# A ring of twelve 14 KB weight slots in place of twenty-one 8 KB slots, with whole-row reads of the expert matrices

## The chip, the cores and the metric

One core of one Trainium2 chip runs the kernel. The metric is device time in microseconds (us) of one execution. Engines are named as in the profile: PE (TensorE matmul), PEld (its weight loads), DVE (VectorE), ACT (ScalarE), POOL (GpSimd) and SP (SyncE), which issues nearly all DMAs. L148 is line 148 of the kernel before.

## The reference

A two-layer backbone over 256 latent and 256 context tokens of width 1024, in float32. Layer 0 is attention beside a convolution module and then a dense feed-forward network; layer 1 is a state-space mixer and then a mixture of experts over the 256 latent tokens alone:

```python
logits = (hf @ w_router).astype(jnp.float32)
top_v, top_i = lax.top_k(logits, TOP_K)              # 2 of 8
gates = ...                                          # softmax of the two, zero elsewhere
for e in range(N_EXPERTS):                           # w1, w3: 1024 x 3584, w2: 3584 x 1024
    out = out + gates[:, e:e + 1] * swiglu(hf, w1[e], w3[e], w2[e])
```

`swiglu` is (silu(h w1) * (h w3)) w2. A final RMSNorm follows. Each matrix of an expert has 14.68 MB, an expert 44.04 MB, all eight 352.3 MB.

## The kernel before

**Order of the program.** Phases 1 and 2 compute layer 0 and the mixer of layer 1 (to about 1052 us in the profile). `route` picks the two experts of each token, `gather` (L1486, L1492, L1494) collects the tokens of an expert as columns of `xe`, and `experts` runs the eight experts. Experts 1 to 7 are taken in an order by token count, with fixed room for 3, 2, 3, 2, 3, 2, 3, 1 groups of 32 tokens (`GROUPS`); call that the number of groups.

**An expert.** The 3584 hidden columns are cut in two slices, 4 x 512 columns and 4 x 384 columns (`SS`). `up(s, i, name)` multiplies the tokens with slice s of w1 (i = 0) or w3 (i = 1): for each of the 8 blocks of 128 rows, and for each group, four matmuls side by side in the four column strips of the array (L1533). ACT takes the silu of the first product (L1541), DVE multiplies it by the second (L1544). `turn(s)` transposes the result (L1566), `down(s)` multiplies it with the rows of w2 (L1598). `evict` copies the sums, `scatter` (L1622, L1627) adds them to the tokens. Order within expert e: both up of slice 0, scatter of expert e-1, turn(0), both up of slice 1, gather of expert e+1, turn(1), down(0), down(1).

**The weight pieces and their ring.** A piece is one DMA on SP's queue (L148). Up pieces are 128 rows by 2048 columns (1 MiB, runs of 8 KB) or by 1536 columns (0.75 MiB, runs of 6 KB); down pieces are 1 MiB with two rows of w2 per partition (runs of 8 KB), two pieces of each expert with two separate rows (runs of 4 KB). An expert has 32 up pieces and 14 down pieces. They go round 21 slots of 8 KB a partition: one of its own (`rawe`), nine of `t8p`, three of `rawp`, three of `hlp`, five of `rawm`; each piece, of whatever size, takes one slot, and a slot is free again when the last matmul that reads it is done. `AHEAD` is how many pieces are asked for ahead of the one in use.

**What is in that room in phase 2.** Kilobytes a partition, in order of address: `cp` 11, `rawp` 24, (`rawe` 8), `hlp` 24, `t8p` 72, `ecp` 5, `op` 22, `wp2` 48. `rawp` and `hlp` hold the raw and the split weights of the mixer's output projection, `t8p` its inputs and `g1`, which the residual reads (L806); `ecp` holds `cs` and `op` holds `BT` and `CT`, all read by the router's matmul (L1345); `wp2` holds small work tiles, the last of them read at L1357. `mp`, `rp` and `ep` (routing and expert work tiles) are opened over the room of closed pools: by default a new pool's first use waits for all tiles of the closed pools it overlaps.

**Queues.** An engine runs its instructions in order; that order is written at compile time by a list scheduler from simulated times. SP holds a DMA back until its slot is free and until a DMA eight before it has landed. `km` (slot numbers and group ranks, needed by `places`, L1659) and `g2r` are small DMAs in SP's queue (L1415, L1462).

Of the kernel before, what the change touches and what calls it, by code (L numbers as in the profile page):

```python
# [10 lines left out]
F32 = mybir.dt.float32  # L11
# [79 lines left out]
class Net:  # L91
# [31 lines left out]

    BUFS = {"t8": 9, "t2": 6, "pe": 9, "cv": 4, "g": 3}

# [10 lines left out]
    def load(self, view, pool=None):  # L136

        if isinstance(view, View):
            view = view.get()
        pieces = view if isinstance(view, list) else [(slice(0, P), view)]  # L140
        kk, n = pieces[0][1].shape[1:]
        if pool == "t8":
            t = self.wk([P, 2048], "t8")
# [5 lines left out]
        return v  # L149

    def wparts(self, v, k0, m, scale=None):
# [1355 lines left out]
    def pos_rows(self, pos):  # L1507

        nc = self.nc
        self.pos = pos  # L1510
        pt = self.ps()
        nc.tensor.transpose(pt[:16, 0:P], pos.rearrange("p b e -> p (b e)"), self.ident)
        r = self.wk([16, P], "posr", bufs=1)
        nc.scalar.copy(r, pt[:16, 0:P])
        d = self.drp.tile([16, P], F32, name=self.nm("posd"))
        nc.sync.dma_start(d, r)
        self.posd = d.rearrange("(b e) p -> b e p", b=2)

    def expert(self, e, n_g):
# [3 lines left out]

        def up(s, i, name):
            c0, n = self.SS[s]

            def begin():
                st[i] = [self.ps("h") for _ in range(n_g)]

            def mm(k, wv, _):  # L1530
                for g in range(n_g):
                    for p in range(4):
                        nc.tensor.matmul(st[i][g][32 * p:32 * p + 32, :n], st["x"][:, k, 32 * g:32 * g + 32],  # L1533
                                         wv[:, n * p:n * p + n], start=k == 0, stop=k == KD - 1,
                                         tile_position=(0, 32 * p))

            def end():
                if i == 0:
                    st["g"] = [self.wk([P, 512], "g")[:, :n] for _ in range(n_g)]
                    for g in range(n_g):  # L1540
                        nc.scalar.activation(st["g"][g], st[0][g][:, :n], AF.Silu)  # L1541
                else:
                    for g in range(n_g):
                        nc.vector.tensor_mul(st["g"][g], st["g"][g], st[1][g][:, :n])  # L1544

            view = lambda k: self.weights(name, e, [P, 1, 4 * n], lambda w: w[:, k * P:(k + 1) * P, c0:c0 + 4 * n]
                                          .rearrange("o p n -> p o n"))
            return Unit([view(k) for k in range(KD)], mm, begin, end, False)

        def take():  # L1550
            st["x"] = self.xe

        def turn(s):


            n = self.SS[s][1]

            def call():
                st["hT", s] = hT = self.wk([P, n // P, 3, P], f"hT{s}", bufs=1)
                for g in range(n_g):  # L1560
                    pt = self.ps("h")
                    for c in range(n // P):
                        t = st["g"][g][:, c // 2 * 256:c // 2 * 256 + min(256, n - c // 2 * 256)]
                        if t.shape[-1] == 256:
                            t = t.rearrange("p (i j) -> p j i", j=2)[:, c % 2]
                        nc.tensor.transpose(pt[:, c * P:(c + 1) * P], t, self.ident)  # L1566
                    o, i = hT[:, :n // P, g], pt[:, :n].rearrange("p (c t) -> p c t", t=P)
                    if g % 2:
                        nc.vector.tensor_copy(o, i)
                    else:  # L1570
                        nc.scalar.copy(o, i)
            return Unit(begin=call)

        def down(s):
            r0, n = 4 * self.SS[s][0] // 4, self.SS[s][1]
            rows = lambda r, m: (lambda w: w[:, r:r + m])
            pair = lambda w: w.rearrange("o (i j) n -> i (o j) n", j=2)
# [12 lines left out]
            def begin():  # L1590
                if s == 0:
                    st["y"] = [self.ps("y") for _ in range(0, n_g, 2)]

            def mm(k, wv, _):
                p, c = pieces[k // 2][1][k % 2]
# [8 lines left out]
            return Unit([self.weights("od_ex_w2", e, [P, 2, D], f) for f, _ in pieces], mm, begin,  # L1604
                        evict if s else None, False)
# [9 lines left out]
        def scatter():  # L1615
# [8 lines left out]
            for b in range(2):  # L1624
# [61 lines left out]
    def experts(self, n_g, now=None):  # L1686
# [21 lines left out]

    AHEAD = 20

# [9 lines left out]
    def moe(self):  # L1720
# [4 lines left out]
        self.run(self.experts(GROUPS, self.late), self.AHEAD)  # L1725
        self.fn = self.wk([P, D], "t8")
        nc.sync.dma_start(self.fn, self.A["final_norm"].partition_broadcast(P))
        self.o = self.wk([P, 2, D], "t8")
        self.finish()

        with self.tc.If(self.over > 0):
            self.rings = [self.rawp]
            for q in (0, 1):
# [10 lines left out]
    def finish(self):  # L1744

        nc = self.nc
        for b in range(2):
            for half in range(2):
                self.sumsq(2 + b, half, "g")
            rs = self.rms_rs(slice(2 + b, 3 + b))  # L1750
# [79 lines left out]
def build(tc, A, out, dbg=None):  # L1830
# [5 lines left out]

    with ExitStack() as ctx, tc.tile_pool(name="cp", bufs=1) as net.cp, \
            tc.tile_pool(name="rawp", bufs=3) as net.rawp, \
            tc.tile_pool(name="rawe", bufs=1) as net.rawe, \
            tc.tile_pool(name="hlp", bufs=3) as net.hlp:  # L1840
        net.drp = ctx.enter_context(tc.tile_pool(name="drp", bufs=1, space=bass.MemoryType.DRAM))
        with tc.tile_pool(name="t8p", bufs=9) as net.t8p, ExitStack() as early:
            net.ecp = early.enter_context(tc.tile_pool(name="ecp", bufs=1))
            with tc.tile_pool(name="xcp", bufs=1) as net.xcp, tc.tile_pool(name="rawx", bufs=1) as net.rawx, \
# [8 lines left out]
            early.close()  # L1853
            with psum("psm", h=6, y=2) as net.psp, tc.tile_pool(name="mp", bufs=1) as net.mp:
                net.t_tag = "h"
                with tc.tile_pool(name="rp", bufs=1) as net.wp:
                    net.route()
                with tc.tile_pool(name="ep", bufs=1) as net.wp, tc.tile_pool(name="rawm", bufs=5) as rawm:
                    net.rings = [net.rawe] + ["t8"] * 9 + [net.rawp] * 3 + [net.hlp] * 3 + [rawm] * 5
                    net.n_ring = -1  # L1860
                    net.moe()

# [12 lines left out]
```

## Time and profile before

| | us |
|---|---|
| median of 3 runs | 1911.31 (1908.12 to 1911.62) |
| the profiled execution | 1911.85 |
| its span | 1910.1 |
| PE busy | 1778.9 (93%) |
| DVE, ACT, POOL busy | 703.5, 519.1, 174.1 |
| read from HBM | 494.45 MB, 259 GB/s over the span |

The span runs from the first to the last profiled instruction; the profiled execution's own time has 1.75 us around it. Matmuls overlap and their ends are modelled, so a busy PE need not be working at its peak. A float32 matmul is two records. Where PE waits between two groups of matmuls, the row says in brackets how long and for whom.

### The profile page before, as it was taken

How to read it: one execution, taken by the hardware profiler on the slowest of the kernel's cores; microseconds unless marked ns; L12 is line 12 of the kernel's file. 1: busy time of each engine (PE TensorE's matmuls, PEld its weight loads, DVE VectorE, ACT ScalarE, POOL GpSimd, SP SyncE). 2: the span in 40 equal slices, each digit the busy share in tenths (PEclk: the TensorE clock that was granted, in tenths of full speed). 3: DMA queues.
4: the chain of work that ended last, by engine and by line, in shares of the span. 5: the costliest groups of instructions: out<-in, count | busy, mean ns of one | idle time of the engine just before them, and what ended most of it. 6: DMA issues, size and time to landing. Idle time of an engine off the chain costs nothing. (4 is left out here: it accounts for less than half of the span.)

```text
span 1910.1 us, 33591 instructions
## 1 busy us (share of the span) xinstructions
PE 1778.9 (93%) x14384; PEld 1110.9 (58%) x14384; DVE 703.5 (37%) x1143; ACT 519.1 (27%) x969; POOL 174.1 (9%) x167
## 2 busy tenths in 40 slices
PE   6999998999999989989989999999999999899964
PEld 3675356788888868757667445445644463435411
DVE  3395546334334356798887110101110101002001
ACT  3434454231222335756874100100000000001000
POOL 0064000000000014133320000000000000000000
PEclk8999999999999999989899899999999999999976
DMA  8543765422323243323357899999999999999995
GB/s 319 178 157 120 250 184 189 135 96 89 109 89 98 81 142 103 122 84 115 101 197 279 320 399 418 416 418 416 418 416 417 417 417 412 414 419 413 417 413 230
DMA packets 131574, 497.87 MB, mean 261 GB/s; under 512 B 11312, under 2 KB 18392, under 8 KB 102744
## 3 DMA queue, kind: packets, MB, share of 16 engines
q1 hardware_dynamic: 126808, 487.25, 66.3%
q10 hardware_dynamic: 4608, 8.39, 1.3%
q8 instruction: 115, 1.88, 0.4%
q14 instruction: 43, 0.35, 0.1%
HBM read 494.45 MB, written 1.15 MB: 259 GB/s over the span
## 5 line engine op out<-in xcount | busy, mean ns | idle before, releaser
L1533 PE MATMUL h<-raw,xe 128*32 128x512 f32 (+1 forms) x2664 | 265.6, 551 | 15.8 <-DMA raw<-in_od_ex_w_dram 15.8
L244 PE MATMUL g<-t,whl 128*128 128x512 f32 (+1 forms) x608 | 237.4, 390 | 0.0
L243 PE MATMUL g<-t,whl 128*128 128x512 f32 (+1 forms) x608 | 234.8, 396 | 2.1 <-ACT opad L1057 1.9
L245 PE MATMUL g<-t,whl 128*128 128x512 f32 (+1 forms) x608 | 232.7, 390 | 0.8 <-POOL whl L164 0.8
L1533 PE MATMUL h<-t,xe 128*32 128x384 f32 (+1 forms) x2200 | 214.9, 543 | 7.7 <-DMA t<-in_od_ex_w_dram 7.7
L164 DVE TENSOR_TENSOR whl<-raw,whl 128x1024 fp32r<-128x1024 f32 x109 | 137.7, 1266 | 206.6 <-ACT whl L161 206.1
L161 ACT CAST whl<-raw 128x1024 fp32r<-128x1024 f32 x129 | 134.5, 1049 | 269.9 <-PE g L245 234.3
L1533 PEld LDWEIGHTS h<-raw,xe 128*32 128x32 f32 x2664 | 97.8, 111 | 175.2 <-issue 113.2
L1544 DVE TENSOR_TENSOR g<-g,h 128x512 f32<-128x512 f32 (+1 forms) x38 | 23.6, 621 | 425.9 <-PE h L1533 238.6
L244 PE MATMUL g<-whl,t 128*128 128x512 f32 (+1 forms) x432 | 168.0, 392 | 9.2 <-DVE whl L164 7.3
L245 PE MATMUL g<-whl,t 128*128 128x512 f32 (+1 forms) x432 | 164.4, 389 | 0.0
L243 PE MATMUL g<-whl,t 128*128 128x512 f32 (+1 forms) x432 | 160.5, 394 | 1.9 <-DVE t L641 1.8
L1533 PEld LDWEIGHTS h<-t,xe 128*32 128x32 f32 x2200 | 79.1, 110 | 136.1 <-issue 91.8
L1598 PE MATMUL y<-raw,hT 128*32 128x256 f32 x2512 | 144.7, 388 | 9.7 <-DMA raw<-in_od_ex_w_dram 9.7
L1541 ACT ACTIVATE g<-h 128x512 f32<-128x512 f32 (+1 forms) x38 | 20.7, 544 | 448.9 <-PE h L1533 448.9
L243 PEld LDWEIGHTS g<-t,whl 128*128 128x128 f32 x608 | 116.6, 192 | 29.3 <-ACT opad L1057 2.3
L244 PEld LDWEIGHTS g<-t,whl 128*128 128x128 f32 x608 | 116.3, 191 | 23.7 <-issue 1.0
L245 PEld LDWEIGHTS g<-t,whl 128*128 128x128 f32 x608 | 115.4, 190 | 24.2 <-POOL whl L164 1.0
L428 POOL TENSOR_SCALAR rsv<-sst 128x1 f32<-128x1 f32 (+1 forms) x15 | 4.7, 311 | 1295.0 <-DVE sst L421 1294.8
L1598 PEld LDWEIGHTS y<-raw,hT 128*32 128x32 f32 x2512 | 80.0, 112 | 72.4 <-DMA raw<-in_od_ex_w_dram 15.0
L1598 PE MATMUL y<-t,hT 128*32 128x256 f32 x1744 | 103.4, 395 | 10.7 <-DMA t<-in_od_ex_w_dram 10.7
L1612 DVE TENSOR_TENSOR ys<-y,g2r 128x512 f32<-128x512 f32 (+1 forms) x12 | 6.6, 577 | 260.6 <-PE y L1598 260.6
(349 smaller groups left out, 2091.1 us busy)
## 6 DMA issues: line engine op xcount, KB each, us to landing
raw<-in_od_ex_w_dram SPq DMA_DIRECT2D x138, 1024.0 KB, 18.0
t<-in_od_ex_w_dram SPq DMA_DIRECT2D x102, 1024.0 KB, 19.2
raw<-in_od_ex_w_dram SPq DMA_DIRECT2D x68, 768.0 KB, 15.0
t<-in_od_ex_w_dram SPq DMA_DIRECT2D x60, 768.0 KB, 15.8
raw<-in_ev_ff_w_dram SPq DMA_DIRECT2D x32, 1024.0 KB, 5.1
raw<-in_ev_ada_w_dram SPq DMA_DIRECT2D x24, 1024.0 KB, 6.7
raw<-in_od_ada_w_dram SPq DMA_DIRECT2D x24, 1024.0 KB, 5.2
raw<-in_od_w_in_dram SPq DMA_DIRECT2D x20, 1024.0 KB, 5.2
```

The costliest lines, as they stand in the source:

```text
L161: self.nc.scalar.copy(hv, v[:, k0:k0 + m])
L164: eng.tensor_tensor(lv, v[:, k0:k0 + m], hv.bitcast(F32), op=ALU.subtract)
L243: mm(out, l[0], r[0], start=start, stop=False)
L244: mm(out, l[0], r[1], start=False, stop=False)
L245: mm(out, l[1], r[0], start=False, stop=stop)
L428: nc.gpsimd.tensor_scalar(v[:, :m], ss, inv_n, EPS, op0=ALU.mult, op1=ALU.add)
L1533: nc.tensor.matmul(st[i][g][32 * p:32 * p + 32, :n], st["x"][:, k, 32 * g:32 * g + 32], wv[:, n * p:n * p + n], start=k == 0, stop=k == KD ...
L1541: nc.scalar.activation(st["g"][g], st[0][g][:, :n], AF.Silu)
L1544: nc.vector.tensor_mul(st["g"][g], st["g"][g], st[1][g][:, :n])
L1598: nc.tensor.matmul(st["y"][g // 2][32 * q:32 * q + 32, g % 2 * 256:g % 2 * 256 + 256], st["hT", s][:, c, g, 32 * p:32 * p + 32], wv[:, 256 ...
L1612: nc.vector.tensor_tensor(ys[:, g:g + m], st["y"][g // 2][:, :256 * m].rearrange("p (g n) -> p g n", g=m), self.g2.unsqueeze(1).to_broadca ...
```

## The change

The pools `rawp`, `hlp`, `t8p` and `ecp` are closed after phase 2, `rawe` and `rawm` are gone, and a pool `big` of twelve slots of 14 KB a partition is opened in their place, with waits by tile: a slot waits only for the tiles that lay where it lies. An up piece is now 128 whole rows of w1 or w3 (1.75 MiB, runs of 14 KB), both slices at once; a down piece has two rows per partition in slice 0 (1 MiB, runs of 8 KB, 8 pieces) and three in slice 1 (1.5 MiB, runs of 12 KB, 4 pieces). An expert has 16 up pieces and 12 down pieces. Order within expert e: both up, scatter of expert e-1, gather of expert e+1, turn(0), turn(1), down(0), down(1). `AHEAD` goes from 20 to 12. `g` is a tile per slice, the row of positions shares the tile `prow`, and the final norm's vector and the output use slots s3 and s4.

```diff
-        def up(s, i, name):
-            c0, n = self.SS[s]
-
+        def up(i, name):
             def begin():
-                st[i] = [self.ps("h") for _ in range(n_g)]
+                st[i] = [[self.ps("h") for _ in self.SS] for _ in range(n_g)]
 
             def mm(k, wv, _):
                 for g in range(n_g):
-                    for p in range(4):
-                        nc.tensor.matmul(st[i][g][32 * p:32 * p + 32, :n], st["x"][:, k, 32 * g:32 * g + 32],
-                                         wv[:, n * p:n * p + n], start=k == 0, stop=k == KD - 1,
-                                         tile_position=(0, 32 * p))
+                    for s, (c0, n) in enumerate(self.SS):
+                        for p in range(4):
+                            nc.tensor.matmul(st[i][g][s][32 * p:32 * p + 32, :n], st["x"][:, k, 32 * g:32 * g + 32],
+                                             wv[:, c0 + n * p:c0 + n * p + n], start=k == 0, stop=k == KD - 1,
+                                             tile_position=(0, 32 * p))
...
-            view = lambda k: self.weights(name, e, [P, 1, 4 * n], lambda w: w[:, k * P:(k + 1) * P, c0:c0 + 4 * n]
+            view = lambda k: self.weights(name, e, [P, 1, 3584], lambda w: w[:, k * P:(k + 1) * P]
                                           .rearrange("o p n -> p o n"))
...
+        RJ = (2, 3)
...
             for p in range(4):
-                for c in range(n // 256):
-                    f = rows(r0 + n * p + 256 * c, 256)
-                    pieces.append((lambda w, f=f: pair(f(w)), [(p, 2 * c), (p, 2 * c + 1)]))
-            if n % 256:
-                for p in (0, 2):
-                    f = rows(r0 + n * p, 2 * n)
-                    pieces.append((lambda w, f=f: f(w).rearrange("o (s i) n -> i (o s) n", s=2)[n - P:n],
-                                   [(p, n // P - 1), (p + 1, n // P - 1)]))
+                for c in range(n // (m * P)):
+                    r = r0 + n * p + m * P * c
+                    pieces.append((lambda w, r=r: w[:, r:r + m * P].rearrange("o (i j) n -> i (o j) n", j=m),
+                                   [(p, m * c + j) for j in range(m)]))
...
-        return ([Unit(begin=take), up(0, 0, "od_ex_w1"), up(0, 1, "od_ex_w3")],
-                [turn(0), up(1, 0, "od_ex_w1"), up(1, 1, "od_ex_w3")], [turn(1), down(0), down(1)],
+        return ([Unit(begin=take), up(0, "od_ex_w1"), up(1, "od_ex_w3")], [turn(0), turn(1), down(0), down(1)],
                 Unit(begin=scatter))
...
-            a, b, c, d = self.expert(e, n_g[e])
-            units += a + scatter + b + gather(e + 1) + c
+            a, b, d = self.expert(e, n_g[e])
+            units += a + scatter + gather(e + 1) + b
...
-    AHEAD = 20
+    AHEAD = 12
...
-                with tc.tile_pool(name="ep", bufs=1) as net.wp, tc.tile_pool(name="rawm", bufs=5) as rawm:
-                    net.rings = [net.rawe] + ["t8"] * 9 + [net.rawp] * 3 + [net.hlp] * 3 + [rawm] * 5
+        with psum("psm", h=6, y=2) as net.psp, \
+                tc.tile_pool(name="big", bufs=1, reuse_waits="tile") as net.big, \
+                tc.tile_pool(name="mp", bufs=1) as net.mp:
+            net.t_tag = "h"
+            for i in range(12):
+                net.slot_tile([P, 3584], f"s{i}")
+            with tc.tile_pool(name="rp", bufs=1) as net.wp:
+                net.route()
+            with tc.tile_pool(name="ep", bufs=1) as net.wp:
+                net.rings = [f"s{i}" for i in (4, 5, 6, 7, 3, 8, 9, 11, 10, 0, 1, 2)]
```

## Rows read from the trace of the kernel before

**Rows 1.** The page: DMA busy tenths of 40 slices, all packets by size, instruction queues.
```profile
DMA  8543765422323243323357899999999999999995
...
DMA packets 131574, 497.87 MB, mean 261 GB/s; under 512 B 11312, under 2 KB 18392, under 8 KB 102744
...
q8 instruction: 115, 1.88, 0.4%
q14 instruction: 43, 0.35, 0.1%
```

**Rows 2.** Windows: start:end, length, busy PE, PEld, DVE, ACT, POOL, PEclk, DMA share, GB/s.
```profile
1066.00:1110.00 44.00, 44.00 (x397) 14.50 (x390) 5.22 (x22) 4.15 (x7) 0.00 (x0) 0.97 0.84 294
1110.00:1141.00 31.00, 31.00 (x384) 12.64 (x387) 1.22 (x2) 2.13 (x5) 0.00 (x0) 1.00 1.01 419
1141.00:1889.00 748.00, 705.61 (x8965) 342.25 (x8961) 73.22 (x170) 39.81 (x82) 0.00 (x0) 0.97 1.01 414
```

**Rows 3.** Waits of SP's queue, 1066 to 1112 us: us in total, times, longest.
```profile
SPq L148 <- PE h L1533: 25.4, 11, 6.9
```

**Rows 4.** Timeline of PE, 1056 to 1150 us (expert 0): start, us, instruction, count.
```profile
1065.20 4.46 PE L1533 MATMUL h<-raw,xe 128*32 128x512 f32 x24
1069.49 18.20 PE L1533 MATMUL h<-t,xe 128*32 128x512 f32 x168
...
1108.71 1.75 PE L1566 MATMUL h<-ka,g 128*128 128x128 f32 x12
1110.39 11.82 PE L1533 MATMUL h<-raw,xe 128*32 128x384 f32 x144
...
1141.49 3.79 PE L1486 MATMUL h<-pm,h 128*128 128x64 f32 x32
...
1146.28 4.09 PE L1598 MATMUL y<-raw,hT 128*32 128x256 f32 x72
```

**Rows 5.** Timeline of PE, 1780 to 1850 us (up pieces of expert 7).
```profile
1810.07 1.07 PE L1533 MATMUL h<-raw,xe 128*32 128x512 f32 x8 [1.42 <-DMA raw<-in_od_ex_w_dram]
...
1824.99 1.74 PE L1533 MATMUL h<-t,xe 128*32 128x512 f32 x8 [0.57 <-DMA t<-in_od_ex_w_dram]
...
1832.49 0.85 PE L1533 MATMUL h<-t,xe 128*32 128x384 f32 x8 [0.21 <-DMA t<-in_od_ex_w_dram]
...
1849.48 0.85 PE L1533 MATMUL h<-raw,xe 128*32 128x384 f32 x8 [1.03 <-DMA raw<-in_od_ex_w_dram]
```

**Rows 6.** Timelines of PE: last down piece of expert 3 and of expert 7.
```profile
1463.27 1.93 PE L1598 MATMUL y<-raw,hT 128*32 128x256 f32 x32 [0.60 <-DMA raw<-in_od_ex_w_dram]
...
1891.29 1.93 PE L1598 MATMUL y<-raw,hT 128*32 128x256 f32 x16 [1.45 <-DMA raw<-in_od_ex_w_dram]
```

**Rows 7.** Timeline, 1045 to 1070 us: the last readers of g1, CT and wp2's tiles.
```profile
1047.25 0.74 DVE L806 SCALAR_TENSOR_TENSOR yt<-g,rs,t 128x512 f32<-128x512 f32 x1
...
1050.98 0.64 PE L1345 MATMUL t<-CT,cs 128*32 128x256 f32 x8
...
1052.81 0.36 DVE L1357 SCALAR_TENSOR_TENSOR L<-t,rs,rbias 128x8 f32<-128x8 f32 x2 [0.70 <-PE t L1351]
```

**Rows 8.** Timeline of SP's DMA issues, 970 to 1070 us.
```profile
1034.33 0.84 SPq L148 DMA_DIRECT2D t<-in_od_ex_w_dram  x2
...
1051.71 0.33 SPq L1415 DMA_DIRECT2D km<-in_kc_dram  x1
```

**Rows 9.** DMA issues, 1066 to 1112 us: count, KB each, median us to landing.
```profile
t<-in_od_ex_w_dram SPq DMA_DIRECT2D x9, 768.0 KB, 4.4
```

**Rows 10.** DMA packets of 1360 to 1380 us and of 1286 to 1306 us.
```profile
DMA packets 1144, 8.36 MB, mean 418 GB/s; under 512 B 126, under 2 KB 126, under 8 KB 126
...
DMA packets 1508, 8.32 MB, mean 416 GB/s; under 512 B 167, under 2 KB 167, under 8 KB 1471
```

**Rows 11.** Timeline of DVE, 1058 to 1068 us.
```profile
1062.92 0.38 DVE L1494 TENSOR_SCALAR xe<-h,m2o,ac 128x96 f32<-128x96 f32 x1 [2.89 <-ACT xe L1492]
1063.22 0.20 DVE L1659 TENSOR_TENSOR ranked<-rank,km 128x49 f32<-128x49 f32 x1
```

More of the change, by code (lines that the diff above doesn't have):

```diff
@@ L122, in ps @@
         return self.psp.tile([P, 512], F32, tag=tag, name=self.nm(tag), bufs=self.psum_tags.get(tag))
-    BUFS = {"t8": 9, "t2": 6, "pe": 9, "cv": 4, "g": 3}
+    BUFS = {"t8": 9, "t2": 6, "pe": 9, "cv": 4, "g0": 3}
     def wk(self, shape, tag, dt=F32, bufs=None, pool=None):
@@ L141, in load @@
         kk, n = pieces[0][1].shape[1:]
-        if pool == "t8":
-            t = self.wk([P, 2048], "t8")
+        if isinstance(pool, str):
+            t = self.slot_tile([P, 3584], pool)
         else:
@@ L149, in load, with slot_tile @@
         return v
+    def slot_tile(self, shape, tag):
+        return self.big.tile(shape, F32, tag=tag, name=self.nm(tag))
     def wparts(self, v, k0, m, scale=None):
@@ L1512, in pos_rows @@
         nc.tensor.transpose(pt[:16, 0:P], pos.rearrange("p b e -> p (b e)"), self.ident)
-        r = self.wk([16, P], "posr", bufs=1)
+        r = self.wk([P, 256], "prow", bufs=1)[:16, :P]
         nc.scalar.copy(r, pt[:16, 0:P])
@@ L1522, in expert @@
         st = {}
-        def up(s, i, name):
-            c0, n = self.SS[s]
+        def up(i, name):
             def begin():
-                st[i] = [self.ps("h") for _ in range(n_g)]
+                st[i] = [[self.ps("h") for _ in self.SS] for _ in range(n_g)]
             def mm(k, wv, _):
                 for g in range(n_g):
-                    for p in range(4):
-                        nc.tensor.matmul(st[i][g][32 * p:32 * p + 32, :n], st["x"][:, k, 32 * g:32 * g + 32],
-                                         wv[:, n * p:n * p + n], start=k == 0, stop=k == KD - 1,
-                                         tile_position=(0, 32 * p))
+                    for s, (c0, n) in enumerate(self.SS):
[3 more added lines that the diff above has]
+                                             tile_position=(0, 32 * p))
             def end():
                 if i == 0:
[L1539 to L1544, printed above, removed]
-            view = lambda k: self.weights(name, e, [P, 1, 4 * n], lambda w: w[:, k * P:(k + 1) * P, c0:c0 + 4 * n]
+                    st["g"] = [[self.wk([P, n], f"g{s}", bufs=3) for s, (_, n) in enumerate(self.SS)]
+                               for _ in range(n_g)]
+                for g in range(n_g):
+                    for s, (_, n) in enumerate(self.SS):
+                        t, q = st["g"][g][s], st[i][g][s][:, :n]
+                        if i == 0:
+                            nc.scalar.activation(t, q, AF.Silu)
+                        else:
+                            nc.vector.tensor_mul(t, t, q)
+            view = lambda k: self.weights(name, e, [P, 1, 3584], lambda w: w[:, k * P:(k + 1) * P]
                                           .rearrange("o p n -> p o n"))
@@ L1551, in take @@
             st["x"] = self.xe
+        RJ = (2, 3)
         def turn(s):
-            n = self.SS[s][1]
+            n, m = self.SS[s][1], RJ[s]
             def call():
@@ L1562, in call @@
                     for c in range(n // P):
[L1563 to L1566, printed above, removed]
+                        t = st["g"][g][s][:, c // m * m * P:(c // m + 1) * m * P]
+                        nc.tensor.transpose(pt[:, c * P:(c + 1) * P], t.rearrange("p (i j) -> p j i", j=m)[:, c % m],
+                                            self.ident)
                     o, i = hT[:, :n // P, g], pt[:, :n].rearrange("p (c t) -> p c t", t=P)
@@ L1574, in down @@
         def down(s):
-            r0, n = 4 * self.SS[s][0] // 4, self.SS[s][1]
-            rows = lambda r, m: (lambda w: w[:, r:r + m])
-            pair = lambda w: w.rearrange("o (i j) n -> i (o j) n", j=2)
+            (r0, n), m = self.SS[s], RJ[s]
             pieces = []
             for p in range(4):
-                for c in range(n // 256):
-                    f = rows(r0 + n * p + 256 * c, 256)
-                    pieces.append((lambda w, f=f: pair(f(w)), [(p, 2 * c), (p, 2 * c + 1)]))
-            if n % 256:
-                for p in (0, 2):
-                    f = rows(r0 + n * p, 2 * n)
-                    pieces.append((lambda w, f=f: f(w).rearrange("o (s i) n -> i (o s) n", s=2)[n - P:n],
-                                   [(p, n // P - 1), (p + 1, n // P - 1)]))
+                for c in range(n // (m * P)):
+                    r = r0 + n * p + m * P * c
+                    pieces.append((lambda w, r=r: w[:, r:r + m * P].rearrange("o (i j) n -> i (o j) n", j=m),
+                                   [(p, m * c + j) for j in range(m)]))
             def begin():
@@ L1594, in mm @@
             def mm(k, wv, _):
-                p, c = pieces[k // 2][1][k % 2]
+                p, c = pieces[k // m][1][k % m]
                 for g in range(n_g):
@@ L1602, in mm @@
                                          tile_position=(0, 32 * q))
-            return Unit([self.weights("od_ex_w2", e, [P, 2, D], f) for f, _ in pieces], mm, begin,
+            return Unit([self.weights("od_ex_w2", e, [P, m, D], f) for f, _ in pieces], mm, begin,
                         evict if s else None, False)
@@ L1725, in moe @@
         self.run(self.experts(GROUPS, self.late), self.AHEAD)
-        self.fn = self.wk([P, D], "t8")
+        self.fn = self.slot_tile([P, 3584], "s3")[:, :D]
         nc.sync.dma_start(self.fn, self.A["final_norm"].partition_broadcast(P))
-        self.o = self.wk([P, 2, D], "t8")
+        self.o = self.slot_tile([P, 3584], "s4")[:, :2 * D].rearrange("p (b n) -> p b n", b=2)
         self.finish()
         with self.tc.If(self.over > 0):
-            self.rings = [self.rawp]
+            self.rings = ["s0", "s1", "s2"]
             for q in (0, 1):
@@ L1748, in finish @@
             for half in range(2):
-                self.sumsq(2 + b, half, "g")
+                self.sumsq(2 + b, half, "g0")
             rs = self.rms_rs(slice(2 + b, 3 + b))
@@ L1835, in psum @@
         return tc.tile_pool(name=name, bufs=2, space=PSUM)
[L1837 to L1840, printed above, removed]
+    with ExitStack() as ctx, tc.tile_pool(name="cp", bufs=1) as net.cp:
         net.drp = ctx.enter_context(tc.tile_pool(name="drp", bufs=1, space=bass.MemoryType.DRAM))
-        with tc.tile_pool(name="t8p", bufs=9) as net.t8p, ExitStack() as early:
-            net.ecp = early.enter_context(tc.tile_pool(name="ecp", bufs=1))
+        with tc.tile_pool(name="rawp", bufs=3) as net.rawp, tc.tile_pool(name="hlp", bufs=3) as net.hlp, \
+                tc.tile_pool(name="t8p", bufs=9) as net.t8p, tc.tile_pool(name="ecp", bufs=1) as net.ecp:
             with tc.tile_pool(name="xcp", bufs=1) as net.xcp, tc.tile_pool(name="rawx", bufs=1) as net.rawx, \
@@ L1852, in build @@
                 net.phase2(h)
[L1853 to L1857, printed above, removed]
-                with tc.tile_pool(name="ep", bufs=1) as net.wp, tc.tile_pool(name="rawm", bufs=5) as rawm:
-                    net.rings = [net.rawe] + ["t8"] * 9 + [net.rawp] * 3 + [net.hlp] * 3 + [rawm] * 5
-                    net.n_ring = -1
-                    net.moe()
+        with psum("psm", h=6, y=2) as net.psp, \
[8 more added lines that the diff above has]
+                net.rings = [f"s{i}" for i in (4, 5, 6, 7, 3, 8, 9, 11, 10, 0, 1, 2)]
+                net.n_ring = -1
+                net.moe()
 def kernel(**inputs):
```

## The prediction, made before the changed kernel ran

> **What bounds the kernel now.** I read the page first, then a table of windows over the expert stage, SP's waits, and the timelines around the stage's ends. The page's DMA row [rows 1] shows two programs: up to slice 21 the DMA engines are half idle, from slice 23 on they are full to the end. The windows [rows 2] put the border in the first expert: 294 GB/s from 1066 to 1110 us, then 419 and 414 GB/s until 1889 us. Of those 823 us the first 44 are not DMA-bound, the rest is.
>
> The reader is to see why the 44 us are slow. SP waits 25.4 us for PE to free slots [rows 3]: the ring is full. PE works without a break [rows 4]: expert 0 has three groups, and a 1 MiB up piece is 24 records of 18.20 / 168 = 108.3 ns, 2.60 us. Every slot that it frees held 1 MiB and is filled with a 0.75 MiB piece; 0.786 MB per 2.60 us is 302 GB/s, the rate found.
>
> The price of a piece in the DMA-bound part is best read in expert 7, whose single group makes PE wait for every piece [rows 5]: six intervals of 8 KB runs in 14.92 us are 2.487 us a piece, nine intervals of 6 KB runs in 16.99 us are 1.888 us. From the last piece of expert 3 to that of expert 7 [rows 6] are 428.02 us, 107.0 an expert; back from 1463.27, expert 0's last piece landed at about 1142.3 us. An expert by pieces is 16 x 2.487 + 16 x 1.888 + 12 x 2.487 + 2 x 2.53 = 104.9 us; 2.1 us an expert I can't place.
>
> **The change part by part.**
>
> *Longer rows.* The two prices differ by 0.599 us per 2 KB of run. Drawn on, a 14 KB piece takes 2.487 + 3 x 0.599 = 4.284 us (428 GB/s), a 12 KB piece 3.685. An expert becomes 16 x 4.284 + 8 x 2.487 + 4 x 3.685 = 103.2 us: 1.7 less, 11.9 us over experts 1 to 7, which are DMA-bound. That rows of 14 KB go out whole no row shows, but 8 KB ones do: the packets not under 8 KB [rows 1] are 131574 - 102744 = 28830, which is 224 DMAs x 128 rows + 115 + 43 instruction packets. Bounds: no gain (long rows are cut), and 24 us (the 2.1 us vanish too).
>
> [...]
>
> *The ring of twelve and expert 0.* Expert 0's 12 down pieces fill the ring exactly. So expert 1's first piece can't start until PE has used expert 0's first down piece, while before, the DMA was through with expert 0 at 1142.3 us and went on without a gap. PE's way there [rows 4]: 16 rows of 24 x 108.3 ns + 24 x 82.1 ns (11.82 / 144) = 4.57 us are 73.1 us; 1.7 us more for the first records (4.29 us against 2.60) and 0.3 for the two small steps in `late`; from 1065.2 that is 1140.3. Gather 3.8, turns 1.75 + 1.24, first down piece 48 x 56.8 ns = 2.7: 1149.8 us. An issue into an empty queue lands 4.4 us later for a 1.89 us piece [rows 9], 2.5 us of delay: what corresponds to 1142.3 is 1152.3, so expert 1 starts 10.0 us later.
>
> Does DMA keep up with PE that far? Slots s4 and s7 are free when the two buffers [rows 8] are, at 1034 us, s6 when the residual's reader of g1 ends at 1048.0, s8 and s9 after the router's matmul at 1051.6 [rows 7]. Expert 0's 103.2 us of DMA end at 1139 if they run from 1036, at 1150 if s5 and s6 hold up the queue until 1047; either way just before the 1152.3. The eight pieces that were loaded before 1034 us (the pair in [rows 8] are the ninth and tenth) are lost without a price, since PE needs row j only at 1065.2 + 4.57 j. In later experts the ring doesn't fill: even with three groups PE is through its first down piece 73.1 + 2.9 + 3.8 + 3.0 + 2.7 = 86 us after it starts, and the DMA needs 103 us for the expert.
>
> *Order and banks.* Each up of three groups now takes all six h banks, so w3's first matmul waits for the silu of w1's first bank. That bank is complete 0.87 us into the last row, 3.7 us before it is wanted: 0. Both turns stand together before down: hT copies hide behind the second turn, 0 to 0.7 us in expert 0, nothing elsewhere (PE waits there for DMA). Scatter moves behind both up; its sums are 100 us old by then: 0.
>
> *SP and small DMAs.* 28 issues of 0.35 us an expert instead of 46: SP has slack. The final norm's vector waits for s3, which the fourth-last piece leaves; the sums, the scatter and the squares hide it. Gone from the start of the kernel is one 1 MiB load (0 to -2.5 us; PE doesn't wait for it, I take 0).
>
> *The end.* The last piece is 1.5 MiB: 24 records instead of 16 behind the last landing. 16 take 1.93 us [rows 6]: +1.0 us.
>
> **Sum** against the profiled execution's own 1911.85 us: + 10.0 - 11.9 + 1.0 = -0.9, 1911.0; that execution stands 0.5 above the median, so 1910.4.
>
> **The rivals.**
> - *The unplaced time goes too* (faster). For it: 6 KB stretches in later experts are slower than in expert 7's good ones, and 414 GB/s over all [rows 2] is below 418 for 8 KB runs [rows 10]. Against: the small DMAs and instruction loads stay. At its most, 427 GB/s on long rows and 420 on 8 KB ones, an expert takes 103.5 us instead of 107.0: 10 + 1 - 24.5 = -13.5, 1898. Half of what I can't place gives 10 + 1 - 11.9 - 7 x 1.05 = -8.3: 1903.
> - *Rows matter little* (slower). The windows of [rows 10] make it 320 / 1018 = 314.3 ns an 8 KB packet and (320 - 37 x 0.314) / 1304 = 236.5 ns a 6 KB packet (16 engines x 20 us): a slope of 77.8 ns per 2 KB leaves 3 ns a packet that length can't touch, where expert 7 gives 11. Then an expert goes from 105.8 to 105.2 us, 4.2 us in seven: 10 + 1 - 4.2 = +6.8, 1918. Cut rows give +11, 1922. [...]
> - *`km` comes late* (slower). `mp` now lies over `wp2` and waits for all of it, so `km` is issued after 1053.2 [rows 7] instead of 1051.71 [rows 8], behind up to eight DMAs of 4.28 us: it lands at 1075 to 1090 us instead of before 1063.2. On DVE, L1659 needs it, and three of the four L1494 that write `xe` stood behind L1659 [rows 11]. If they still do, PE stops at its fourth row, at 1065.2 + 13.7 = 1079. From a landing after 1077 each us is one us of the end, as expert 0's way is all PE: up to 12, taken as +8, 1918. Against it: the list scheduler, which placed L1659 behind an L1494 before, is likely to place it behind all of them when `km` is later still.
> - *The waits aren't by tile* (slower): if all slots open only at 1053.2 us, expert 0's DMA ends at 1055.5 + 103.2 = 1158.7, plus a landing of about 2 us against 1152.3: +8, 1918.
>
> **How the numbers follow.** The forecast has 0.40; the faster rival 0.32; rows that matter little 0.13, `km` 0.10, waits by pool 0.05: slower 0.28. A measurement of this kernel can't tell less than 0.2%, 3.8 us, from no change, and the forecast's -0.9 is inside; the other cases are outside on their sides. Time 1910.4. The range reaches to 1898 and 1922, the most that the faster rival gives and cut rows; outside lie the worst of `km` and two rivals at once. The forecast's own range is 1906 to 1915.
>
> **What would show it.** Right: a ring that is full through expert 0 with PE unbroken from 1065 to 1150 us; a DMA gap of a few us before about 1152; packets of 14 and 12 KB; PE in expert 7 waiting 4.28 us a row piece and 3.69 a 12 KB piece; about 105.3 us an expert; expert 0's first row still at 1065 us. Wrong: row pieces of 4.38 us or more, or of 4.2 or less; DVE idle before L1659 while `xe` is unfinished; expert loads that begin after 1053 us; or any gap in DMA after expert 1, which would mean that twelve slots are too few.

## The result, and the profile after

The changed kernel takes 1923.23 us (median of four runs, 1922.36 to 1926.01) against 1911.46 for the kernel before: ratio 1.0063, 95% interval 1.0041 to 1.0084. It is slower by 12 us. I had forecast 1910.4, within 0.2% of before, and the time lies 1.2 us above the range. The profiled execution has a span of 1920.9 us, 10.8 more than before.

The page of the kernel after: DMA busy tenths, and packets by size.
```profile
DMA  7443765323223233423441999999999999999995
...
DMA packets 108785, 497.82 MB, mean 259 GB/s; under 512 B 9008, under 2 KB 16088, under 8 KB 79960
```
Against [rows 1] the packets fall by 22789, and those not under 8 KB number 28825, which is 224 DMAs x 128 rows + 115 + 38 instruction packets: rows of 12 and 14 KB go out whole. But slice 22 now has a 1 where before it had a 7: the DMA engines stand nearly still ahead of the expert stage.

Windows of the kernel after (columns as in [rows 2]).
```profile
1034.00:1045.00 11.00, 9.24 (x44) 7.12 (x42) 5.63 (x9) 3.13 (x7) 0.00 (x0) 1.00 0.00 0
1045.00:1066.00 21.00, 16.79 (x106) 12.76 (x110) 9.89 (x58) 8.09 (x15) 0.90 (x2) 0.67 0.60 234
1066.00:1110.00 44.00, 44.00 (x471) 15.29 (x467) 0.17 (x1) 3.40 (x7) 0.00 (x0) 1.00 1.01 426
1110.00:1141.00 31.00, 31.00 (x321) 14.18 (x314) 5.85 (x13) 2.41 (x6) 0.00 (x0) 1.00 1.01 421
1141.00:1889.00 748.00, 698.65 (x8855) 338.07 (x8853) 70.02 (x166) 36.84 (x79) 0.00 (x0) 0.99 1.01 422
```
The stage around 1066 to 1110 us, which the prediction called slow, has gone from 294 to 426 GB/s, and the long DMA-bound part from 414 to 422. Yet no byte moves from 1034 to 1045 us. From about 1055 us to the end the DMA engines never rest: the ring does not stall, which the prediction expected it to.

Why, the timeline of SP's DMA issues says (1000 to 1112 us, kernel after), and its waits over 1011 to 1112 us (us in total, times, longest).
```profile
1003.57 7.86 SPq L148 DMA_DIRECT2D raw<-in_od_w_out_dram  x2
1050.86 0.35 SPq L1418 DMA_DIRECT2D km<-in_kc_dram  x1
1051.26 1.82 SPq L1465 DMA_DIRECT2D g2r<-drow  x4
1053.12 55.94 SPq L148 DMA_DIRECT2D s<-in_od_ex_w_dram  x20
```
```profile
SPq L148 <- DMA s<-in_od_ex_w_dram: 46.1, 12, 4.7
SPq L1418 <- DVE L L1360: 39.2, 1, 39.2
```
`km`, a DMA of 18 numbers a partition, is the next in SP's queue after the mixer's weights, and it waits 39.2 us for L1360, the last reader of `wp2`'s tiles (L1357 before). All expert loads stand behind it. In the kernel before, `km` stood behind sixteen expert loads, the ten up to the pair of [rows 8] and six more, and waited 3.3 us itself. The last of the six in the timeline of SP's DMA issues, and the wait, kernel before:
```profile
1048.02 0.33 SPq L148 DMA_DIRECT2D t<-in_od_ex_w_dram  x1
```
```profile
SPq L1415 <- PE t L1345: 3.3, 1, 3.3
```

PE, kernel after: expert 0, the last down piece of expert 3, and in expert 7 up rows, down pieces of 8 KB and of 12 KB runs, the last scatter.
```profile
1062.64 12.66 PE L1535 MATMUL h<-s,xe 128*32 128x512 f32 x132
...
1141.61 36.49 PE L1598 MATMUL y<-s,hT 128*32 128x256 f32 x672
...
1478.62 1.72 PE L1598 MATMUL y<-s,hT 128*32 128x256 f32 x28 [0.94 <-DMA s<-in_od_ex_w_dram]
...
1845.16 1.71 PE L1535 MATMUL h<-s,xe 128*32 128x512 f32 x16 [1.38 <-DMA s<-in_od_ex_w_dram]
...
1866.64 1.71 PE L1535 MATMUL h<-s,xe 128*32 128x512 f32 x16 [2.61 <-DMA s<-in_od_ex_w_dram]
...
1871.60 1.07 PE L1598 MATMUL y<-s,hT 128*32 128x256 f32 x16 [0.47 <-DMA s<-in_od_ex_w_dram]
...
1886.49 1.07 PE L1598 MATMUL y<-s,hT 128*32 128x256 f32 x16 [0.89 <-DMA s<-in_od_ex_w_dram]
1890.32 2.79 PE L1598 MATMUL y<-s,hT 128*32 128x256 f32 x24 [2.75 <-DMA s<-in_od_ex_w_dram]
...
1901.30 2.79 PE L1598 MATMUL y<-s,hT 128*32 128x256 f32 x24 [0.91 <-DMA s<-in_od_ex_w_dram]
1904.63 2.09 PE L1622 MATMUL h<-ys,PT 32*128 32x256 f32 x16 [0.55 <-DVE ys L1612]
```
The reader is to see three things. Five intervals of 14 KB rows take 21.48 us, 4.296 a piece (forecast 4.284); six of 8 KB 14.89, 2.482 (2.487); three of 12 KB 10.98, 3.66 (3.685). From expert 3 to expert 7 are 422.68 us, 105.67 an expert against 107.0 [rows 6]. And back from 1478.62 by three of these, expert 0's last piece landed at 1161.6, where before it was 1142.3.

Executions begin their expert stage at different moments: the changed kernel and three of the experiments below, with the same order of matmuls on PE through phases 1 and 2, have the first up row (the first matmuls of expert 0's first up piece) at 1062.64, 1062.45, 1068.03 and 1068.76 us. So I compare profiles from the first up row of expert 0. To the last down piece of expert 7 it is 826.1 us before [rows 4, 6] and 838.7 after, to the last scatter 828.6 and 842.0.

| kernel | us, median | ratio to before (95%) | to last down piece | to last scatter |
|---|---|---|---|---|
| after | 1923.23 | 1.0063 (1.0041 to 1.0084) | 838.7 | 842.0 |
| `mp` by tile | 1913.10 | 1.0000 (0.9986 to 1.0015) | 826.0 | 828.1 |
| `km` from ACT | 1913.32 | 1.0016 (1.0002 to 1.0030) | 828.2 | 831.5 |
| `mp` by tile, ring by pool | 1924.12 | 1.0043 (1.0018 to 1.0067) | 837.7 | 841.1 |
| by tile, slots in ready order | 1910.78 | 0.9990 (0.9975 to 1.0004) | 825.9 | 829.2 |
| the same, early down | 1909.58 | 0.9985 (0.9970 to 1.0000) | 825.3 | 828.6 |
| ready order, ring of ten | 1920.44 | 1.0056 (1.0039 to 1.0072) | 835.2 | 838.5 |
| after, rows cut 8 + 6 KB | 1937.31 | 1.0131 (1.0109 to 1.0154) | 849.0 | 852.3 |
| after, rows in two halves | 2490.05 | 1.3019 (1.2953 to 1.3086) | | |
| after, even and odd rows | 1927.57 | 1.0091 (1.0077 to 1.0106) | 839.2 | 842.5 |
| ready order, ten down pieces | 1904.50 | 0.9962 (0.9948 to 0.9975) | | 822.5 |
| the same, early down | 1901.91 | 0.9954 (0.9941 to 0.9968) | | 819.4 |

Each ratio is to runs of the kernel before made beside that kernel (medians of 1909.73 to 1911.46 us), and is not the quotient of two medians.

### The profile page after: what moved, and what is told of

It reads as the page before. It is cut to its first block, busy times and chain, and to the rows that moved or that the text cites. A ratio compares the mean times of both kernels' runs of the same rounds, so it can differ in the third digit from the quotient of the medians.

```text
span 1920.9 us, 33036 instructions
## 1 busy us (share of the span) xinstructions
PE 1779.6 (93%) x14384; PEld 1112.5 (58%) x14384; DVE 701.2 (37%) x1143; ACT 517.0 (27%) x969; POOL 175.0 (9%) x167
## 5 line engine op out<-in xcount | busy, mean ns | idle before, releaser
L1535 PE MATMUL h<-s,xe 128*32 128x512 f32 (+1 forms) x4864 | 469.8, 543 | 29.1 <-DMA s<-in_od_ex_w_dram 28.9
L1535 PEld LDWEIGHTS h<-s,xe 128*32 128x32 f32 x4864 | 158.2, 110 | 328.4 <-issue 280.9
L1598 PE MATMUL y<-s,hT 128*32 128x256 f32 x4256 | 243.7, 388 | 23.9 <-DMA s<-in_od_ex_w_dram 23.5
L1598 PEld LDWEIGHTS y<-s,hT 128*32 128x32 f32 x4256 | 148.8, 112 | 115.7 <-DMA s<-in_od_ex_w_dram 30.3
L247 PEld LDWEIGHTS g<-whl,t 128*128 128x128 f32 x432 | 82.7, 192 | 30.4 <-DVE whl L167 8.5
L246 PEld LDWEIGHTS g<-whl,t 128*128 128x128 f32 x432 | 82.0, 191 | 28.9 <-issue 4.5
L248 PEld LDWEIGHTS g<-whl,t 128*128 128x128 f32 x432 | 82.9, 192 | 17.8 <-issue 2.2
```

Of the source, the lines that this page charges most:

```text
L246: mm(out, l[0], r[0], start=start, stop=False)
L247: mm(out, l[0], r[1], start=False, stop=False)
L248: mm(out, l[1], r[0], start=False, stop=stop)
L1535: nc.tensor.matmul(st[i][g][s][32 * p:32 * p + 32, :n], st["x"][:, k, 32 * g:32 * g + 32], wv[:, c0 + n * p:c0 + n * p + n], start=k == 0, ...
```

## The experiments

**Is it the wait of `km`?** One word is added: the pool of `km` waits by tile. The order of all matmuls on PE stays.
```diff
-                tc.tile_pool(name="mp", bufs=1) as net.mp:
+                tc.tile_pool(name="mp", bufs=1, reuse_waits="tile") as net.mp:
```


> The changed kernel with one word more: the pool mp, which holds km, also waits by tile. Theory (km at the head of SP's queue holds back every expert load for 39.2 us, to 1053.1): km goes out before 1025, the first two expert loads before 1030, the rest from about 1044.7 when the residual's last reader of g1 (L809) is done; expert 0's DMA ends near 1142, PE is then the limit, and expert 1's first piece goes out when PE has used expert 0's first down piece, at 1144.2, with its data 2.5 us later. Back-projected from expert 3 the DMA is through with expert 0 at 1161.6 in the changed kernel, so 14 us come back: 1909 (1907 to 1912). Rival A (the ring of twelve is the limit in expert 0 whatever the loads do): no DMA time comes back, 1922 to 1924. Rival B (the slots don't open one by one): km goes early, but the first expert load still at 1050 to 1053: 1921 to 1924.

Ratio 1.0000 instead of 1.0063, and 826.0 us instead of 838.7. SP's issues (two views), a window with the stall of the ring, and PE:
```profile
1011.37 0.42 SPq L1418 DMA_DIRECT2D km<-in_kc_dram  x1
...
1144.30 22.35 SPq L148 DMA_DIRECT2D s<-in_od_ex_w_dram  x9
```
```profile
1031.00 27.96 SPq L148 DMA_DIRECT2D s<-in_od_ex_w_dram  x12
```
```profile
1141.00:1150.00 9.00, 9.00 (x165) 6.28 (x167) 1.44 (x4) 0.96 (x3) 0.00 (x0) 1.00 0.85 317
```
```profile
1062.45 36.29 PE L1535 MATMUL h<-s,xe 128*32 128x512 f32 x384
...
1465.73 2.80 PE L1598 MATMUL y<-s,hT 128*32 128x256 f32 x48 [0.95 <-DMA s<-in_od_ex_w_dram]
...
1888.46 1.50 PE L1598 MATMUL y<-s,hT 128*32 128x256 f32 x24 [0.90 <-DMA s<-in_od_ex_w_dram]
```
`km` goes out 39.5 us earlier, the twelve first loads go out from 1031.00 instead of 1053.12, and expert 1's first load at 1144.30, when PE has used expert 0's first down piece. The ring's stall of the prediction is there, 317 GB/s from 1141 to 1150 us. Rivals A and B are out. The first loads came later than I wrote (one at 1031.00, the next at 1041.95), and the gain in time was 10 to 12 us instead of 14: the median of 1913.10 us lies above the 1907 to 1912 that I gave.

**Is it the place in SP's queue?** `km` and `g2r` are issued by ACT; `mp` waits for the pools as before.
```diff
-        nc.sync.dma_start(km, self.A["kc"][:, NCONST:])
+        nc.scalar.dma_start(km, self.A["kc"][:, NCONST:])
...
-            nc.sync.dma_start(self.g2[32 * i:32 * i + 32], g2[256 * i:256 * i + 256].partition_broadcast(32))
+            nc.scalar.dma_start(self.g2[32 * i:32 * i + 32], g2[256 * i:256 * i + 256].partition_broadcast(32))
```


> The changed kernel with km and g2r issued from ACT's queue; mp still waits for the whole closed pools, so km goes out no earlier than before (about 1051). Theory (it is the place at the head of SP's in-order queue that costs, not the wait itself): SP's expert loads start near 1030 as with mp by tile, and from the first up row of expert 0 to the last down piece of expert 7 PE needs 826 us as there, against 838.7 in the changed kernel; 1910 to 1914. Rival (mp's wait for the whole pool is what costs, through km's late landing or the other tiles of mp): 838 us, 1922 to 1924.

Issues of this kernel, 1035 to 1075 us, and one of SP's waits:
```profile
1038.08 36.16 SPq L148 DMA_DIRECT2D s<-in_od_ex_w_dram  x12
1057.64 0.36 ACTq L1418 DMA_DIRECT2D km<-in_kc_dram  x1
```
```profile
SPq L148 <- DMA km<-in_kc_dram: 13.9, 1, 13.9
```
`km` is as late as it was (12.0 us ahead of the first up row, in the changed kernel 11.8), and the loads start 19.6 us before it all the same: 828.2 us. The rival falls. Where the other 2.2 us are wasn't tested; the likely place is the wait above. One expert load was held back 13.9 us until `km` had landed, and near the end of that wait DMA fell to a third (the same kernel's window):
```profile
1063.00:1069.00 6.00, 6.00 (x30) 6.00 (x30) 3.23 (x23) 0.43 (x1) 0.00 (x0) 0.50 0.47 137
```

**Do the ring's waits by tile matter?**
```diff
-                tc.tile_pool(name="big", bufs=1, reuse_waits="tile") as net.big, \
-                tc.tile_pool(name="mp", bufs=1) as net.mp:
+                tc.tile_pool(name="big", bufs=1) as net.big, \
+                tc.tile_pool(name="mp", bufs=1, reuse_waits="tile") as net.mp:
```


> As the kernel with mp by tile, but the ring's pool (big) waits by pool, which is my rival of the prediction in the pure form. Theory (both waits must be by tile; the first expert load then waits itself for the last reader of the closed pools, L1360 at 1050.7): expert loads from about 1050.8, 2 us earlier than in the changed kernel since km and g2r are out of the way: 1921 to 1923. If waits by tile on the ring bring nothing, it equals the kernel with mp by tile alone (1909 by the theory).

837.7 us, and in the waits the same line stands in front of the loads themselves:
```profile
SPq L148 <- DVE L L1360: 36.9, 1, 36.9
```
So the slots do open one by one, and in the changed kernel that was worth nothing, because `km` kept the queue shut for as long. In the trace this wait alone costs 11.7 of the 12.7 us. The runs are less sharp: they spread from 1913.98 to 1928.79 us, with a median above the 1921 to 1923 expected, but the ratio (1.0018 at the least) is above that with `mp` by tile alone (1.0015 at the most).

**What is the bound once `km` is out of the way?** The slots are taken in the order in which they come free.
```diff
-                net.rings = [f"s{i}" for i in (4, 5, 6, 7, 3, 8, 9, 11, 10, 0, 1, 2)]
+                net.rings = [f"s{i}" for i in (4, 7, 0, 3, 5, 2, 1, 6, 11, 8, 9, 10)]
```


> As the kernel with mp by tile, and the slots are taken in the order in which they come free (s4, s7, s0, s3, s5, s2, s1, s6, s11, s8, s9, s10); the order of instructions on PE, DVE, ACT and POOL is unchanged. Theory: loads run from about 1024 with a gap to 1036 and are steady from 1036 to 1042, 5 to 8 us more of DMA before 1053, but expert 1's first piece still waits for PE's first down piece at 1144.2: the same time as with mp by tile alone, within 2 us (1909). Rival (expert 0 is DMA-bound there, the loads' start sets the end): 5 to 8 us less, 1901 to 1904.

825.9 us against 826.0. Earlier loads bring nothing, the ring's wait for PE is the bound. The time, 0.9990, is no different from 1.0000 within the intervals.

Then PE is brought earlier to the first down piece (beside ready order):
```diff
-            units += a + scatter + gather(e + 1) + b
+            units += a + scatter + [b[0], b[2]] + gather(e + 1) + [b[1], b[3]]
```


> As the kernel with the slots in the order in which they come free, and the order within an expert is turn(0), down(0), gather of the next expert, turn(1), down(1), so that PE reaches the first down piece earlier: the scheduler leaves about half of the gather (9 of 16 parts, 2.1 of 3.8 us) ahead of it and moves turn(1) (1.2 us) behind. Theory (PE's way to the first down piece sets the start of expert 1's loads): 2.9 us less than that kernel, 1906. Rival (expert 0 is DMA-bound): no difference to it.

825.3 us, only 0.6 less: inconclusive. In this execution expert 0's first 384 records took 38.00 us against 36.29, which eats 1.7 of the 2.9 us: the granted clock was still 0.50 in the 3 us from the first up row, where `mp` by tile, with 36.29 us as well, has 1.00 in its first 2 us (1062.45 to 1064.45 us).
```profile
1064.47:1067.47 3.00, 3.00 (x18) 0.80 (x21) 1.17 (x4) 2.14 (x3) 0.00 (x0) 0.50 1.01 430
```

And the ring is cut to ten slots (`[:10]` behind the list, `AHEAD = 10`):


> The kernel with mp by tile and the slots in the order in which they come free, with ten slots instead of twelve. Theory (expert 1's first piece waits for the slot of the piece that lies a ring before it): it now waits for expert 0's third down piece instead of its first, 2 x 2.6 = 5.2 us later, and nothing else stalls: from the first up row of expert 0 to the last down piece of expert 7 PE needs 831 us instead of 825.9; 1915 to 1917. Rival (twelve slots are more than the ring needs): 826, 1910 to 1912.

835.2 us: 9.3 more, not 5.2. The rival falls, but the size was wrong. Expert 1's first load (SP's timeline, ten slots), and the last down piece of expert 3 with ten slots and with twelve:
```profile
1151.02 2.93 SPq L148 DMA_DIRECT2D s<-in_od_ex_w_dram  x2
```
```profile
1475.41 2.80 PE L1598 MATMUL y<-s,hT 128*32 128x256 f32 x48 [0.89 <-DMA s<-in_od_ex_w_dram]
```
```profile
1472.09 2.80 PE L1598 MATMUL y<-s,hT 128*32 128x256 f32 x48 [0.95 <-DMA s<-in_od_ex_w_dram]
```
The load goes out 87.0 us after the first up row instead of 81.8, the 5.2 us expected. But expert 3's last piece comes 8.1 us later (411.4 us after the first up row instead of 403.3), so most of the rest is lost before it too. The likely reason, not tested: expert 0's last two down pieces now wait for PE as well (they go out at 1145.84 and 1148.43 us) and are still under way. Experts 4 to 7 add only 1.2 us, though "nothing else stalls" doesn't hold there:
```profile
1550.00:1600.00 50.00, 50.00 (x813) 35.32 (x809) 10.98 (x27) 3.22 (x8) 0.00 (x0) 1.00 0.98 407
1750.00:1800.00 50.00, 50.00 (x673) 32.30 (x669) 10.01 (x23) 3.53 (x8) 0.00 (x0) 0.93 0.95 392
```
With twelve slots these windows, in later experts of three groups, have 423 and 421 GB/s. Bytes that a window lacks needn't be time at the end: these two lack as many as 1.9 and 3.4 us would move, and cost 1.2 us at most.

**What do long rows bring?** Each up piece of the changed kernel is read by two DMAs into its slot. `c` runs over columns 0 to 2048 and 2048 to 3584:
```diff
-            self.nc.sync.dma_start(v[sl], src)
+            self.nc.sync.dma_start(v[sl][:, :, c], src[:, :, c])
```


> The changed kernel with each up piece read by two DMAs into the same slot, one with the runs of 8 KB of slice 0 and one with the runs of 6 KB of slice 1, which are the run lengths of the kernel before; DMA-bound from 1055 us to the end, so the price of a piece counts for all eight experts. Theory (the length of the run sets the price, 2.482 + 1.888 us against the 4.296 measured in expert 7): 16 x 0.074 = 1.2 us an expert, 9.5 in eight: 1932 to 1933. Rival (a packet has a fixed 3 ns, as 'rows matter little' of the prediction): 0.4 us an expert, 3 in eight: 1926.

849.0 us, 10.3 more than after, where the price of the pieces gives 9.5 and the fixed 3 ns a packet 3; the median of 1937.31 us is above the 1932 to 1933 expected. The last down pieces of expert 3 and of expert 7:
```profile
1492.49 2.80 PE L1598 MATMUL y<-s,hT 128*32 128x256 f32 x48 [0.95 <-DMA s<-in_od_ex_w_dram]
...
1920.49 2.79 PE L1598 MATMUL y<-s,hT 128*32 128x256 f32 x24 [0.91 <-DMA s<-in_od_ex_w_dram]
```
That is 428.00 us, 107.0 an expert, the same as in the kernel before [rows 6]. A control needs as many DMAs with rows left whole; `c` runs over partitions 0 to 63 and 64 to 127 (`v[sl][c]`):


> The control to the kernel with cut rows: as many DMAs as there, two for each up piece, but each of 64 partitions and whole rows of 14 KB. If the run's length is what costs there, this one is as the changed kernel: 1923 to 1925. If it is the number of DMAs (issues, and the wait for the eighth before), it is as slow as the one with cut rows.

It takes 2490 us and is no control. The window 1070 to 1180 us:
```profile
1070.00:1180.00 110.00, 72.10 (x623) 25.78 (x619) 0.17 (x1) 3.40 (x7) 0.00 (x0) 0.88 1.01 214
```
All DMA engines are busy and move 214 GB/s, half of the 426 after. My guess was that it is the half of the partitions to which each DMA goes; how that would halve the rate no run shows. The control anew, with even and odd partitions (`slice(0, P, 2)`, `slice(1, P, 2)`):


> The control to the kernel with cut rows, done anew: two DMAs for each up piece, whole rows of 14 KB, one for the even and one for the odd partitions (the DMAs of 64 neighbouring partitions moved 214 GB/s with all 16 DMA engines busy). Theory (with cut rows it was the length of the run that cost 10 us, and what halved the rate was that a DMA went to one half of the partitions): as the changed kernel, 1923 to 1926, 838.7 us of PE from the first up row of expert 0 to the last down piece of expert 7. Rival A (the number of DMAs is what costs): as with cut rows, 849 us, 1933 to 1937. Rival B (any DMA of 64 partitions is slow): near 2490.

839.2 us, 0.5 more than after: twice the DMAs, and 64 partitions in each, cost next to nothing in the expert stage. The median of 1927.57 us is 4.3 above the changed kernel's and outside the 1923 to 1926 expected; in the profiles the difference lies ahead of the stage (first up row at 1067.61 us instead of 1062.64), and no run shows why. With rows cut it was the run's length that cost 9.8 us of the 10.3.

**A version that beats both.** If the ring's wait for PE is what is left, fewer pieces per expert must help: w2 in ten pieces instead of twelve, slice 1 first, slice 0 as four pieces of three rows per partition and two of separate rows; `mp` by tile, ready order.
```diff
-            for p in range(4):
-                for c in range(n // (m * P)):
...
+            pieces = [(lambda w, r=r0 + n * p: w[:, r:r + 384].rearrange("o (i j) n -> i (o j) n", j=3),
+                       [(p, 0), (p, 1), (p, 2)]) for p in range(4)]
+            if n > 384:
+                pieces.append((lambda w: w[:, r0:r0 + 3 * n].rearrange("o (s i) n -> i (o s) n", s=3)[n - P:n],
+                               [(p, 3) for p in range(3)]))
+                pieces.append((lambda w: w[:, r0 + 4 * n - P:r0 + 4 * n].rearrange("o i n -> i o n"), [(3, 3)]))
```


> The kernel with mp by tile and the slots in the order in which they come free, and w2 in ten pieces instead of twelve: slice 1 first, then slice 0 with three rows per partition (four pieces of 12 KB runs), one piece of three blocks of 128 separate rows (4 KB runs) and a last one of one block (0.5 MiB). The ring then holds the last two up rows of w3 and the ten down pieces, so expert 1's first two loads wait for PE's 15th and 16th w3... that is, w3's last two rows, instead of the first two down pieces. Theory (the ring's wait for PE in expert 0 is what is left of the loss): two loads of 4.3 us can go before the first down piece is used; the third waits for a first down piece that takes 4.0 us instead of 2.6: expert 1's stream is 8.6 - 1.4 = 7.2 us further on. PE's time from the first up row of expert 0 to the last down piece of expert 7 falls from 825.9 to about 818, the tail behind the last landing shrinks by 1.9 us (8 records instead of 24): 0.9 times 10 us less than with twelve pieces, 1900 to 1903, where the kernel before has 1910 to 1911. Rival (expert 0 is bound by its own DMA, so earlier slots bring nothing): only the tail, 1908 to 1909.

Expert 1's first three loads (three views of SP's timeline); the first up row is at 1065.78 us.
```profile
1134.16 0.35 SPq L148 DMA_DIRECT2D s<-in_od_ex_w_dram  x1
...
1138.67 0.34 SPq L148 DMA_DIRECT2D s<-in_od_ex_w_dram  x1
...
1148.82 0.33 SPq L148 DMA_DIRECT2D s<-in_od_ex_w_dram  x1
```
They come 68.4, 72.9 and 83.0 us after the first up row, with twelve pieces the first at 81.8 (1150.60 less 1068.76). To the last scatter it is 822.5 us instead of 829.2, and the kernel is faster than before, by 0.4%: 0.9962 (0.9948 to 0.9975). The gain is 6.7 us instead of the 9 expected, and the median of 1904.50 us lies above the 1900 to 1903 expected. With the early down besides:


> As the kernel with ten down pieces, and turn(1), down(1), gather of the next expert, turn(0), down(0) in this order. The third load of expert 1 waits for the first down piece, which comes one turn (1.4 us) and about half of the gather (1.7 us) earlier. Theory: up to 3 us less than with ten pieces alone, 1898 to 1902; if the DMA of expert 0 has become the bound by then, no difference.

819.4 us and 0.9954 (0.9941 to 0.9968): the fastest, 3.1 us less in the trace than with ten pieces alone; in time the two intervals overlap.

## Why the prediction was wrong

The step that failed is in "The ring of twelve and expert 0", under "Does DMA keep up with PE that far?": the loads were to run from 1036 us, or from 1047 if s5 and s6 held up the queue. I looked for what holds up the queue among the loads alone. In the rival on `km` I saw that its pool now waits for all of `wp2`, and then put it "behind up to eight DMAs" in SP's queue. It stands in front of them. Expert loads that begin after 1053 us were among the prediction's signs of being wrong; they began at 1053.12. The rival "The waits aren't by tile" has such a start too; its price, +8, was two thirds of the 12.8 below, and its mechanism was another: the waits of the ring are by tile.

From the first up row to the last scatter the changed kernel needs 13.4 us more. Its parts, by the prediction's terms:

| term | forecast | measured | from |
|---|---|---|---|
| ring, expert 0 | +10.0 | +9.1 | `mp` by tile: 1465.73 less three experts of 105.68 is 1148.7, 86.2 after the first up row; before 77.1 |
| `km` | 0 | +12.8 | after: 1161.6 is 99.0 after the first up row, less 86.2 |
| longer rows | -11.9 | -9.3 | 7 x (107.0 - 105.67) |
| the end | +1.0 | +0.9 | 3.33 us from the last piece to the scatter, before 2.48 |
| sum | -0.9 | +13.5 | |

The profiled span grew by 10.8 and not by 13.4, since this execution began the stage 2.6 us earlier.

*Longer rows* were right, with prices within 1% of those drawn on from 6 and 8 KB, and the experiment with cut rows confirms them. The gain came out smaller, 1.33 us an expert (107.0 to 105.67) and not 1.7, since the 2.1 us an expert that I couldn't place didn't stay as they were: 105.67 against 103.2 by pieces leaves 2.4. (The prediction's bound of 24 us for this term is 26.6 by its own numbers, 7 x 3.8; nothing hung on it.) The packets of 1478 to 1584 us, about one expert of the kernel after, show most of it:
```profile
DMA packets 4395, 44.87 MB, mean 423 GB/s; under 512 B 473, under 2 KB 765, under 8 KB 765
```
The weights of 106 us are 44.18 MB; 0.69 MB of other traffic are 1.6 us at that rate; the other 0.8 us stay open. So the faster rival, in which this time goes too, is out. "Rows matter little" is out as well: its 3 ns a packet would make the cut rows cost 3 us, and they cost 9.8. From 8 to 14 KB a packet grows from 310 to 537 ns (2.482 and 4.296 us a piece of 128 packets on 16 engines), 75.6 per 2 KB, which leaves an estimated 8 ns that length can't touch.

*The ring* was right in mechanism, but hidden: with loads that begin 22 us late, the DMA comes to expert 1 after PE has freed its slot. The twelve slots' bound shows as soon as `km` is out of the way, and the kernel then takes what the forecast said, 1.0000 of before. That its size was so near, 9.1 against 10.0, is partly luck. With `mp` by tile PE is through the first down piece 81.9 us after the first up row and not 84.6, and the DMA's start on expert 1, by the same reckoning back from expert 3, follows 4.4 us later and not 2.5. Of the 84.6, 1.7 us were the slow first records of the kernel before, which had a granted clock of 0.50; with `mp` by tile they have 1.00. The first 2 us of the first up row, kernel before and `mp` by tile:
```profile
1065.20:1067.20 2.00, 2.00 (x13) 0.60 (x16) 1.43 (x9) 1.43 (x3) 0.00 (x0) 0.50 1.01 418
```
```profile
1062.45:1064.45 2.00, 2.00 (x25) 0.72 (x28) 1.17 (x4) 1.43 (x3) 0.00 (x0) 1.00 1.00 430
```
*The end* was right at the granted clock of 0.50 that the last down piece has before (16 records in 1.93 us) and after (24 in 2.79 us); with `mp` by tile the 24 take 1.50 us, and the end 2.05 us. *Order and banks*: PE runs without a break in expert 0, as forecast. Of SP and the small DMAs, costed at nothing, `km` was the exception, and *`km` late on DVE* didn't occur: PE goes unbroken through its first rows.

## What to carry to other kernels

Before the bytes of a change are priced, list every instruction of the issuing queue in its order, the small ones too, each with what it waits for: a DMA of 9 KB with a pool-wide wait of 39 us at the head of the queue made the loads of 352 MB behind it begin 22 us later. Here finer waits paid nothing as long as one coarse wait was left in the same queue (838.7 and 837.7 us with one, 826.0 with none). A ring's reach counts in pieces: ten down pieces instead of twelve gave 6.7 us with the same twelve slots.

## What was not expected of the hardware

- Two DMAs for partitions 0 to 63 and 64 to 127 moved 214 GB/s with all 16 DMA engines shown busy; two for even and odd partitions lost next to nothing (839.2 against 838.7 us).
- Whole rows of 14 KB ran at 427 GB/s (1.835 MB in 4.296 us).
- The moment at which phases 1 and 2, with the same matmuls in the same order, are done differs from one profiled execution to another by up to 6 us (first up row at 1062.45 to 1068.76 us), half of the effect studied here; from the first up row on, kernels with the same bound agree within 0.2 us (826.0 and 825.9). The granted clock of the whole execution is 0.969 and 0.968 in the two early ones, 0.961 and 0.964 in the two late ones. Why it differs no run shows.
